# Fourteen operand tiles begin 16 to 240 bytes further on, each at a place of its own

## The chip, the cores and the metric

The kernel runs on one core of a Trainium2 chip. The time is device microseconds from launch to end, as the median of several executions. Four engines compute: PE (TensorE, matrix products into PSUM; its weight loads are shown as PEld), DVE (VectorE), ACT (ScalarE) and POOL (GpSimd). SP (SyncE) and POOL issue transfers.

## The reference

One encoder block on 512 tokens of 1024 channels. After a norm, one projection feeds three mixers: a bidirectional mLSTM, a neighbourhood attention on an 8 x 64 grid, and a cross-attention into 256 memory tokens. Their results are merged by gates. The end of the block, which matters here, is

```python
        merged = g_ml * (y_ml @ w_br_ml[l]) + g_na * (y_na @ w_br_na[l]) + g_xa * (y_xa @ w_br_xa[l])
        x = x + merged @ w_out[l]
        x = x + conv_glu_ffn(rms_norm(x, ffn_norm_g[l]), w_ffn_up[l], w_ffn_conv[l], b_ffn_conv[l], w_ffn_down[l])
    return rms_norm(x, final_norm_g)
```

with `conv_glu_ffn(h) = (gelu(dwconv3(a)) * u) @ w_down`, where `a` and `u` are the halves of `h @ w_up`, 2816 channels each. All data are float32.

## The kernel before, in words

Data is kept turned: channels on the 128 partitions, the 512 tokens along the free dimension. A matrix product therefore has a 128 x 128 block of weights as stationary operand and a 128 x 512 slice of data as moving operand. To keep float32 accuracy, each operand is split into a high part (rounded to the type fp32r) and a low part (the rest), and each product is made of three matmuls into one PSUM bank, in `mm3` (lines 213 to 215): high weights by high data, high weights by low data, low weights by high data. The program loads the weights for each of the three anew, so every matmul has its weight load, which overlaps the matmul before.

Weights come in blocks of up to 1088 floats per partition (`emit_raw`, three buffers), one DMA each on SP's queue. `emit_split` cuts a block into halves of up to 576 floats, high by ACT (line 195) and low by DVE (line 196), four buffers of each. Three blocks ahead are loaded and one ahead is split.

The large data tiles come from one pool of 15 buffers, `unit` (line 130): 2112 floats wide, of which four slices of 512 floats hold data and 64 floats are left over. 2112 floats are 33 x 256 bytes, a weight half of 576 floats is 9 x 256, a raw block of 1088 floats is 17 x 256. A slice of data lies 2048 bytes behind the slice before, a block of weights 512 bytes behind the block before. So, modulo 256 bytes, a unit's slices and the weights' blocks all begin at one place. There are two exceptions, both for 256 columns: `HI256 = 48` floats, 192 bytes, are left free ahead of the high weights of the third token-major block (line 189, where the weights are the moving operand), and ahead of the high weights of the last two output tiles (`lastw`, line 169).

The end of the program is written out in its final order, and the framework adds the semaphores:

- The gates' products are summed in two units. `split_act` (lines 219 and 220: ACT makes the high part, DVE the low one) writes the merged sum into four units, `mhu` (line 1227): high and low of k = 0 to 3, then high and low of k = 4 to 7. They are the moving operand of the output projection, the loop over 8 output tiles f.
- In that loop each tile gets the residual added (line 1244) and is split into four units, `h2` (line 1236), in the same arrangement. They are the moving operand of both halves of the up projection.
- The feed-forward is done in two halves of 11 channel tiles (`for hh in range(2)`, line 1389). Each half takes six units, `gu` (line 1390): three for the high part, three for the low. For each of its 11 tiles there are two up products (`ua`, `uu`, 8 k each), a convolution of three taps, a gelu, a product with `u`, and a split into `gu`. After that the down projection of the half takes `gu` as moving operand: 8 output tiles of 11 k in the first half; in the second half 5 of them, and then `last_tiles`, which works on halves of the tokens and uses `gu` on either side.

Of the kernel before, what the change touches and what calls it, by code (L numbers as in the profile page):

```python
# [12 lines left out]
F32R = mybir.dt.float32r  # L13
# [97 lines left out]
def hybrid_block(ctx, tc, xg, xT, memT, wflat, vecs, gbias, nabias, outa, outb, outc):  # L111
# [14 lines left out]
    def nm(s):  # L126
        uid[0] += 1
        return f"{s}_{uid[0]}"

    def unit(dt=F32):  # L130
        return up.tile([P, UNIT], dt, tag="unit", name=nm("u"))

    def scr(n=512):
        return sp.tile([P, S], F32, tag="scr", name=nm("s"))[:, :n]
# [4 lines left out]
    def mmps():  # L139
        return mmp.tile([P, 512], F32, tag="mm", name=nm("mm"))  # L140
# [60 lines left out]
    def weights(key):  # L201

        i, _, n = BINDEX[key]
        while st["raw"] <= min(i + RAW_AHEAD, len(BLOCKS) - 1):
            emit_raw(st["raw"])
            st["raw"] += 1
        while st["split"] <= min(i + SPLIT_AHEAD, len(BLOCKS) - 1):
            emit_split(st["split"])
            st["split"] += 1
        return split.pop(i)  # L210

    def mm3(ps, lh, ll, rh, rl, start, stop):
        PE.matmul(ps, lh, rh, start=start, stop=False)  # L213
        PE.matmul(ps, lh, rl, start=False, stop=False)  # L214
        st["mm"] = PE.matmul(ps, ll, rh, start=False, stop=stop).ins  # L215

    def split_act(h, l, src, scale=1.0):

        A.activation(h, src, AF.Copy, scale=scale)  # L219
        V.scalar_tensor_tensor(l, src, scale, h.bitcast(F32), op0=ALU.mult, op1=ALU.subtract)  # L220
# [6 lines left out]
    def vcol(name, i):  # L227
        o = VEC[name] + i
        return vec[:, o:o + 1]
# [75 lines left out]
    def folded(acc, ntok):  # L305

        lo, hi = slice(0, P // 2), slice(P // 2, P)
        t, parts = scr(ntok), sp.tile([P, S], F32R, tag="scr", name=nm("s"))[:, :ntok]
        A.activation(t[lo], acc[hi], AF.Copy)
        V.tensor_tensor(t[lo], acc[lo], t[lo], op=ALU.add)  # L310
        A.activation(parts[lo], t[lo], AF.Copy)
        V.tensor_tensor(parts[hi], t[lo], parts[lo].bitcast(F32), op=ALU.subtract)
        return (parts,)

    def square_sums(parts, ntok, pool=atps):

        ps = pool()
        for i, p in enumerate(parts):
            st["mm"] = PE.matmul(ps[:, :ntok], onesr, p, start=i == 0, stop=i == len(parts) - 1).ins
        return ps  # L320
# [12 lines left out]
    def rstd_wide(ps, ntok, tag, n=D):  # L333

        v, y = scr(ntok), scr(ntok)
        rb = cp.tile([P, ntok], F32, name=f"rb_{tag}", tag=f"rb{ntok}", bufs=1) if tag else scr(ntok)
        A.activation(v, ps[:, :ntok], AF.Ln, scale=1.0 / n)
        A.activation(y, v, AF.Exp, scale=-0.5)
        V.scalar_tensor_tensor(v, ps[:, :ntok], -0.5 / n, y, op0=ALU.mult, op1=ALU.mult)
        V.tensor_tensor(v, v, y, op=ALU.mult)  # L340
        V.scalar_tensor_tensor(rb, v, 1.5, y, op0=ALU.add, op1=ALU.mult)
        return rb
# [52 lines left out]
    def proj(key, XHs, XLs, n=S, at={}, ps=None):  # L395

        ws = weights(key)
        k0 = 0 if ps is None else 1
        if ps is None:
            ps = mmps()  # L400
        for k in range(k0, KT):
            mm3(ps[:, :n], ws[k][0], ws[k][1], XHs[k], XLs[k], k == 0, k == KT - 1)
            if k in (1, 3, 5):
                flush()
            if k in at:
                at[k]()
        return ps
# [46 lines left out]
    def conv(ps, rbt, w, b, i, n):  # L454

        pad = pads[npad[0] % 2]
        npad[0] += 1
        V.tensor_tensor(pad[:, 1:513], ps, rbt, op=ALU.mult)  # L458
        t1 = scr()
        A.activation(t1, pad[:, 0:512], AF.Identity, scale=vcol(w, i), bias=vcol(b, i))  # L460
        V.scalar_tensor_tensor(t1, pad[:, 1:513], vcol(w, n + i), t1, op0=ALU.mult, op1=ALU.add)  # L461
        V.scalar_tensor_tensor(t1, pad[:, 2:514], vcol(w, 2 * n + i), t1, op0=ALU.mult, op1=ALU.add)  # L462
        return t1
# [38 lines left out]
    for c in range(3):  # L502
# [10 lines left out]
        for t in range(NT):  # L513
# [3 lines left out]
            if c < 2:  # L517
                o = 16 if c == 0 else 0
# [589 lines left out]
    def step(n=1):  # L1108
        quota[0] += n
        while quota[0] >= 1 and gens:  # L1110
            try:
                next(gens[0])
                quota[0] -= 1
            except StopIteration:
                gens.pop(0)
        if not gens:
            quota[0] = 0.0
# [67 lines left out]
    for br in range(3):  # L1185
# [19 lines left out]
        for fp in range(4):  # L1205
# [18 lines left out]
                    V.scalar_tensor_tensor(tg[i], tg[i], 1.0, ps, op0=ALU.add, op1=ALU.mult)  # L1224
                    V.tensor_tensor(mgv(f), mgv(f), tg[i], op=ALU.add)
            step(1)
    mhu = [unit(F32R) for _ in range(4)]
    GH = [mhu[k // 4 * 2][:, (k % 4) * S:(k % 4 + 1) * S] for k in range(KT)]
    GL = [mhu[k // 4 * 2 + 1][:, (k % 4) * S:(k % 4 + 1) * S] for k in range(KT)]
    for k in range(KT):  # L1230
# [2 lines left out]

    x2u = [unit(), unit()]
    x2 = [x2u[f // 4][:, (f % 4) * S:(f % 4 + 1) * S] for f in range(KT)]
    h2 = [unit(F32R) for _ in range(4)]
    HH = [h2[k // 4 * 2][:, (k % 4) * S:(k % 4 + 1) * S] for k in range(KT)]
    HL = [h2[k // 4 * 2 + 1][:, (k % 4) * S:(k % 4 + 1) * S] for k in range(KT)]
    acc2 = cp.tile([P, S], F32, name="acc_2", tag="acc", bufs=1)
# [147 lines left out]
            SY.dma_start(outc[:, LF * P:], o[:, LF * P:D])  # L1387

    for hh in range(2):
        gu = [unit(F32R) for _ in range(6)]  # L1390
        UH = [gu[k // 4][:, (k % 4) * S:(k % 4 + 1) * S] for k in range(HF)]
        UL = [gu[3 + k // 4][:, (k % 4) * S:(k % 4 + 1) * S] for k in range(HF)]
        for j in range(HF):
            f = HF * hh + j
            if f == 0:
                wa, wu = weights(("ua", f)), weights(("uu", f))
                pa, pu = mmps(), mmps()
                x2sum = folded(acc2, S)
                for k in range(KT):
                    if k < KT - 1:  # L1400
                        mm3(pa, wa[k][0], wa[k][1], HH[k], HL[k], k == 0, False)
                for k in range(KT - 1):
                    mm3(pu, wu[k][0], wu[k][1], HH[k], HL[k], k == 0, False)
                k = KT - 1
                mm3(pa, wa[k][0], wa[k][1], HH[k], HL[k], False, True)
                rb2 = rstd_wide(square_sums(x2sum, S), S, "2")
                mm3(pu, wu[k][0], wu[k][1], HH[k], HL[k], False, True)
                pa1 = proj(("ua", 1), HH, HL)
                pu1 = proj(("uu", 1), HH, HL)
            else:  # L1410
                pa = pa1 if f == 1 else proj(("ua", f), HH, HL)
            c = conv(pa, rb2, "ffw", "ffb", f, FT)
            sq = scr()
            A.activation(sq, c, AF.Square)
            V.scalar_tensor_tensor(sq, sq, GC, c, op0=ALU.add, op1=ALU.mult)  # L1415
            A.activation(sq, sq, AF.Tanh, scale=GK)  # L1416
            V.scalar_tensor_tensor(c, sq, 1.0, c, op0=ALU.add, op1=ALU.mult)  # L1417
            G.tensor_tensor(c, c, rb2, op=ALU.mult)  # L1418
            if f > 0:
                pu = pu1 if f == 1 else proj(("uu", f), HH, HL)  # L1420
            V.tensor_tensor(c, pu, c, op=ALU.mult)  # L1421
            split_act(UH[j], UL[j], c, 0.5)
        for f in range(KT if hh == 0 else LF - 1):
            ws = weights(("dn", hh, f, 0)) + weights(("dn", hh, f, 1))
            ps = mmps()
            for k in range(HF):
                mm3(ps, ws[k][0], ws[k][1], UH[k], UL[k], k == 0, k == HF - 1)
            V.tensor_tensor(x2[f], ps, x2[f], op=ALU.add)  # L1428
            if hh == 1:
                if f == 0:  # L1430
                    with tc.issue_after(A.activation(acc3, x2[f], AF.Square).ins):
                        A.preload_act_table_set("natural_log_exp_and_others")
                else:
                    sq = scr()
                    A.activation(sq, x2[f], AF.Square)
                    G.tensor_tensor(acc3, acc3, sq, op=ALU.add)
                A.activation(x2[f], x2[f], AF.Copy, scale=vcol("fin_g", f))
        if hh == 1:
            last_tiles(UH, UL)
# [114 lines left out]
```

## Time and profile before

| | |
|---|---|
| median of 3 runs | 873.77 us (873.48 to 873.80) |
| profiled execution: span from first to last instruction | 871.2 us |
| PE busy | 865.8 us, 99% of the span, 4287 matmuls |
| DVE, ACT, POOL busy | 594.7, 467.8, 125.4 us |
| mean granted TensorE clock | 1.000 |
| DMA | 99.81 MB, 115 GB/s |

The page gives the span of the profiled execution and no other time for it; the span is the time between first and last instruction, and the runs' times hold what lies around it as well. The chain that ended last is followed back from the last instruction. In the list of groups a line is that of the helper that recorded the instruction, so all split products stand under lines 213 to 215. In the timeline each row has the start in us from the span's start and the duration; PE's rows overlap, since matmuls are pipelined, and the distance from start to start is what a matmul costs. Where that distance is worked out over many rows, the first and the last of them are shown.

### The profile page before, as it was taken

The page shows a single profiled execution, that of the slowest core. Times are in us where ns is not written, and L with a number is a line of the kernel's source. Part 1 is how long each engine was busy: PE and PEld are TensorE (multiplying, and loading weights), DVE is VectorE, ACT ScalarE, POOL GpSimd, SP SyncE. Part 2 cuts the span into 40 slices and gives each one's busy share as a digit, 9 for nine tenths or more (in the row PEclk, how much of TensorE's full clock was granted, in tenths as well). Part 3 has the DMA queues.
Part 4 walks back from the last instruction along what each step waited for, and adds up shares of the span by engine and source line. Part 5 has one row for each costly group of instructions (what it writes and reads, how often), then busy time and mean ns, then how long its engine had stood idle before and what let it go on. Part 6 is the DMA issues. An engine that isn't in the chain of part 4 may idle for free.

```text
span 871.2 us, 12230 instructions
## 1 busy us (share of the span) xinstructions
PE 865.8 (99%) x4287; PEld 733.9 (84%) x4287; DVE 594.7 (68%) x1292; ACT 467.8 (54%) x981; POOL 125.4 (14%) x202
## 2 busy tenths in 40 slices
PE   9999999999999999999999999999999999999997
PEld 7898889888888888888888888888888888888887
DVE  7794698997477768897676558776633466666534
ACT  7563577764355658897534455444422344444532
POOL 0101100000344370600000002111100011111010
PEclk9999999999999999999999999999999999999999
DMA  8324643533343453533223433323233323232412
GB/s 281 101 75 147 196 140 89 169 107 115 93 132 82 113 146 112 160 116 122 99 96 109 144 109 97 98 96 98 78 98 113 102 96 97 96 98 87 141 35 97
DMA packets 39421, 99.81 MB, mean 115 GB/s; under 512 B 5688, under 2 KB 13880, under 8 KB 39360
## 3 DMA queue, kind: packets, MB, share of 16 engines
q1 hardware_dynamic: 31568, 92.32, 32.6%
q0 software_dynamic: 7360, 6.32, 3.4%
q8 instruction: 34, 0.56, 0.3%
q10 hardware_dynamic: 432, 0.39, 0.1%
q14 instruction: 27, 0.22, 0.1%
HBM read 94.80 MB, written 4.21 MB: 114 GB/s over the span
## 4 chain that ended last, share of the span: by engine, by line
PE 98%; DVE 1%; issue 0%; ACT 0%; POOL 0%; POOLq 0%
PE mm L213 29%; PE mm L215 29%; PE mm L214 29%; PE at L214 2%; PE at L213 2%; PE at L215 2%; PE at L982 1%; PE at L963 1%; PE at L944 0%; PE at L945 0%; PE at L765 0%; PE at L813 0%; PE at L1070 0%; PE at L243 0%; PE mm L422 0%
## 5 line engine op out<-in xcount | busy, mean ns | idle before, releaser
L213 PE MATMUL mm<-u,wh 128*128 128x512 f32 (+1 forms) x1072 | 414.3, 386 | 0.0
L215 PE MATMUL mm<-u,wl 128*128 128x512 f32 (+1 forms) x1072 | 411.8, 384 | 0.0
L214 PE MATMUL mm<-u,wh 128*128 128x512 f32 (+1 forms) x1072 | 411.5, 384 | 0.0
L195 ACT ACTIVATE wh<-wr 128x512 fp32r<-128x512 f32 (+2 forms) x298 | 184.2, 621 | 219.9 <-PE mm L214 177.2
L196 DVE TENSOR_TENSOR wl<-wr,wh 128x512 fp32r<-128x512 f32 (+3 forms) x300 | 203.4, 681 | 88.5 <-ACT wh L195 86.4
L215 PEld LDWEIGHTS mm<-u,wl 128*128 128x128 f32 x1072 | 201.3, 188 | 40.3 <-DVE wl L196 0.4
L213 PEld LDWEIGHTS mm<-u,wh 128*128 128x128 f32 x1072 | 201.5, 188 | 39.0 <-ACT wh L195 0.4
L214 PEld LDWEIGHTS mm<-u,wh 128*128 128x128 f32 x1072 | 201.5, 188 | 38.5
L1418 POOL TENSOR_TENSOR s<-s,rb 128x512 f32<-128x512 f32 x22 | 38.2, 1736 | 401.7 <-DVE s L1417 238.9
L540 POOL DMA_DIRECT2D u<-nav_d x128 | 62.5, 535 | 70.5 <-DVE X L220 24.3
L219 ACT ACTIVATE u<-s 128x512 fp32r<-128x512 f32 x26 | 16.4, 632 | 56.4 <-DVE s L1421 56.3
L1421 DVE TENSOR_TENSOR s<-mm,s 128x512 f32<-128x512 f32 x22 | 15.2, 690 | 23.9 <-POOL s L1418 23.9
L460 ACT ACTIVATE s<-pad,vec 128x512 f32<-128x512 f32 x30 | 24.4, 813 | 9.7 <-DVE pad L458 9.7
L220 DVE SCALAR_TENSOR_TENSOR u<-s,u 128x512 fp32r<-128x512 f32 x26 | 19.1, 733 | 14.8 <-ACT u L219 14.5
L461 DVE SCALAR_TENSOR_TENSOR s<-pad,vec,s 128x512 f32<-128x512 f32 x30 | 22.5, 750 | 5.5 <-ACT s L460 5.5
L1417 DVE SCALAR_TENSOR_TENSOR s<-s,s 128x512 f32<-128x512 f32 x22 | 15.2, 691 | 13.4 <-ACT s L1416 13.3
L462 DVE SCALAR_TENSOR_TENSOR s<-pad,vec,s 128x512 f32<-128x512 f32 x30 | 22.5, 750 | 0.9
L1416 ACT ACTIVATE s<-s 128x512 f32<-128x512 f32 x22 | 13.9, 632 | 14.9 <-DVE s L1415 14.9
L1196 DVE TENSOR_TENSOR s<-mm,rb_x 128x512 f32<-128x512 f32 x16 | 11.0, 689 | 13.8 <-PE mm L215 13.7
L458 DVE TENSOR_TENSOR pad<-mm,rb 128x512 f32<-128x512 f32 x22 | 15.1, 690 | 6.4 <-PE mm L215 6.2
L1428 DVE TENSOR_TENSOR u<-mm,u 128x512 f32<-128x512 f32 x13 | 9.0, 692 | 14.6 <-PE mm L215 14.6
L214 PE MATMUL mm<-wl,u 128*128 128x512 f32 x48 | 18.7, 390 | 0.0
(352 smaller groups left out, 1053.3 us busy)
## 6 DMA issues: line engine op xcount, KB each, us to landing
wr<-wflat SPq DMA_DIRECT2D x141, 512.0 KB, 3.3
nab<-nabias SPq DMA_DIRECT2D x16, 256.0 KB, 2.7
u<-nav_d POOLq DMA_DIRECT2D x128, 32.0 KB, 2.8
s<-xT SPq DMA_DIRECT2D x15, 256.0 KB, 4.0
wr<-wflat SPq DMA_DIRECT2D x14, 192.0 KB, 2.4
nav_d<-nv POOLq DMA_DIRECT2D x8, 256.0 KB, 2.5
R<-rd SPq DMA_DIRECT2D x8, 256.0 KB, 4.6
wr<-wflat SPq DMA_DIRECT2D x2, 544.0 KB, 3.4
```

The lines of the kernel that those rows point to most:

```text
L195: A.activation(h[:, u:v], src, AF.Copy)
L196: V.tensor_tensor(l[:, u:v], src, h[:, u:v].bitcast(F32), op=ALU.subtract)
L213: PE.matmul(ps, lh, rh, start=start, stop=False)
L214: PE.matmul(ps, lh, rl, start=False, stop=False)
L215: st["mm"] = PE.matmul(ps, ll, rh, start=False, stop=stop).ins
L219: A.activation(h, src, AF.Copy, scale=scale)
L220: V.scalar_tensor_tensor(l, src, scale, h.bitcast(F32), op0=ALU.mult, op1=ALU.subtract)
L460: A.activation(t1, pad[:, 0:512], AF.Identity, scale=vcol(w, i), bias=vcol(b, i))
L461: V.scalar_tensor_tensor(t1, pad[:, 1:513], vcol(w, n + i), t1, op0=ALU.mult, op1=ALU.add)
L462: V.scalar_tensor_tensor(t1, pad[:, 2:514], vcol(w, 2 * n + i), t1, op0=ALU.mult, op1=ALU.add)
L540: G.dma_start(vw[r * 32:(r + 1) * 32, i * 256:(i + 1) * 256], nav_v[hf, r, CW[b]:CW[b] + 32, hp * 256:(hp + 1) * 256])
L1418: G.tensor_tensor(c, c, rb2, op=ALU.mult)
```

## The change

Fourteen units are used from an offset on, instead of from their first byte. The offsets are, in floats, 40, 56, 8, 4 for the merged gates, 24, 48, 32, 16 for the normalised residual, and 28, 44, 20, 12, 52, 60 for the first feed-forward half: all different, all multiples of 16 bytes, from 16 to 240 bytes. The slices keep their distance of 2048 bytes, and the 64 spare floats of a unit take the offset up. The units of the second feed-forward half keep their place (offset 0), and so do all weights. The instructions, their order and their sizes stay the same.

```diff
-    mhu = [unit(F32R) for _ in range(4)]
+    mhu = [u[:, o:] for u, o in zip([unit(F32R) for _ in range(4)], (40, 56, 8, 4))]
     GH = [mhu[k // 4 * 2][:, (k % 4) * S:(k % 4 + 1) * S] for k in range(KT)]
     GL = [mhu[k // 4 * 2 + 1][:, (k % 4) * S:(k % 4 + 1) * S] for k in range(KT)]
...
-    h2 = [unit(F32R) for _ in range(4)]
+    h2 = [u[:, o:] for u, o in zip([unit(F32R) for _ in range(4)], (24, 48, 32, 16))]
     HH = [h2[k // 4 * 2][:, (k % 4) * S:(k % 4 + 1) * S] for k in range(KT)]
     HL = [h2[k // 4 * 2 + 1][:, (k % 4) * S:(k % 4 + 1) * S] for k in range(KT)]
...
     for hh in range(2):
-        gu = [unit(F32R) for _ in range(6)]
+        gu = [u[:, o:] for u, o in zip([unit(F32R) for _ in range(6)], (28, 44, 20, 12, 52, 60) if hh == 0 else (0,) * 6)]
         UH = [gu[k // 4][:, (k % 4) * S:(k % 4 + 1) * S] for k in range(HF)]
         UL = [gu[3 + k // 4][:, (k % 4) * S:(k % 4 + 1) * S] for k in range(HF)]
```

## The prediction

> **What bounds the kernel now.** The page is read first, from its busy shares (part 1) over the slices (part 2) to the chain that ended last (part 4) and the costliest groups (part 5).
>
> ```profile
> span 871.2 us, 12230 instructions
> PE 865.8 (99%) x4287; PEld 733.9 (84%) x4287; DVE 594.7 (68%) x1292; ACT 467.8 (54%) x981; POOL 125.4 (14%) x202
> ...
> PEclk9999999999999999999999999999999999999999
> ...
> PE 98%; DVE 1%; issue 0%; ACT 0%; POOL 0%; POOLq 0%
> ...
> L213 PE MATMUL mm<-u,wh 128*128 128x512 f32 (+1 forms) x1072 | 414.3, 386 | 0.0
> L215 PE MATMUL mm<-u,wl 128*128 128x512 f32 (+1 forms) x1072 | 411.8, 384 | 0.0
> L214 PE MATMUL mm<-u,wh 128*128 128x512 f32 (+1 forms) x1072 | 411.5, 384 | 0.0
> ```
>
> TensorE never runs dry: 98% of the chain is its own matmuls, the clock is at its full grant in every slice, and the three lines of mm3 show no idle time. So the time is the number of matmuls times the distance from the start of one to the start of the next. That distance is what the change can touch. The mean durations of 384 to 386 ns don't show it, since consecutive matmuls overlap; the timeline does. Next, then, the table by stretches places the four stages whose moving data is shifted, and the timeline of PE inside them gives the distance.
>
> ```profile
> core 0: us, PE busy (x) PEld busy (x) DVE busy (x) ACT busy (x) POOL busy (x), PEclk, DMA share, GB/s
> 459.80:503.50 43.70, 43.70 (x195) 36.18 (x194) 26.42 (x41) 19.21 (x32) 0.00 (x0) 1.00 0.38 126
> 503.50:623.40 119.90, 119.90 (x531) 99.28 (x530) 85.52 (x126) 59.75 (x95) 16.66 (x10) 1.00 0.30 95
> 623.40:683.30 59.90, 59.90 (x266) 49.61 (x265) 21.86 (x34) 15.03 (x26) 1.79 (x1) 1.00 0.34 106
> 683.30:803.00 119.70, 119.70 (x530) 99.12 (x529) 80.69 (x119) 55.63 (x87) 17.95 (x10) 1.00 0.29 92
> ```
>
> ```profile
> start us, us, engine line op out<-in xcount [idle before <-releaser]
> 519.96 0.39 PE L215 MATMUL mm<-u,wl 128*128 128x512 f32 x1
> ...
> 559.86 0.39 PE L214 MATMUL mm<-u,wh 128*128 128x512 f32 x1
> ```
>
> In order: output projection, up projection of the first half, down projection of the first half, up projection of the second half; PE is busy for the whole of each. Between the two timeline rows lie 176 steps of one matmul each: 39.90 us / 176 = 226.7 ns for 512 columns, with DVE and ACT at work beside it and no trace of them.
>
> **The change, part by part.** It adds and removes no instruction, no transfer and no wait; only the addresses of 14 tiles move. Who reads them from TensorE follows from the loops. The merged gates (mhu) are the moving operand of the output projection: 8 tiles x 8 k x 3 = 192 matmuls. The normalised residual (h2) is that of both up projections: 44 x 8 x 3 = 1056. The first feed-forward half (gu, first turn) is that of the first down projection: 8 x 11 x 3 = 264. Together 1512 matmuls, all of 512 columns, out of a stretch of 343 us (459.8 to 803.0). 1512 x 226.7 ns = 342.8 us, so nothing else lies in it.
>
> What the shift does to one matmul is the whole question. Before, units are 33 x 256 bytes wide, weight tiles 9 x 256, and slices start every 512 or 2048 bytes, so the moving slice of each of these matmuls and the weight tile that is loaded for the next begin at the same place modulo 256 bytes. Afterwards the moving data lies 16 to 240 bytes past the weights. The trace has two kinds of matmul that bear on it, neither the same as the changed one.
>
> First, 256 columns. The memory keys run with moving data and weights at one place; in the third token-major block, and in the last tiles, the high halves of the weights lie 192 bytes further on (HI256 = 48 floats).
>
> ```profile
> start us, us, engine line op out<-in xcount [idle before <-releaser]
> 144.11 0.28 PE L214 MATMUL mm<-u,wh 128*128 128x256 f32 x1
> ...
> 145.31 0.28 PE L215 MATMUL mm<-u,wl 128*128 128x256 f32 x1
> ```
>
> ```profile
> start us, us, engine line op out<-in xcount [idle before <-releaser]
> 82.23 0.28 PE L214 MATMUL at<-wl,u 128*128 128x256 f32 x1
> ...
> 92.71 0.28 PE L213 MATMUL at<-wh,u 128*128 128x256 f32 x1
> ```
>
> At one place: 10 steps in 1.20 us, 120.0 ns each. Moved apart: 90 steps in 10.60 us, 117.8 ns. So the place counts, by 2.2 ns. The two widths also give the bare price of a column: (226.7 - 120.0) / 256 = 0.417 ns, so 512 columns cost 213.4 and 256 cost 106.7, and at one place each matmul carries 13.3 ns on top, whatever its width. This steady 13.3 is a settled state, which the second kind shows.
>
> Second, 512 columns at one place, but just after something of another shape (transposes of 128 columns) has broken the stream.
>
> ```profile
> start us, us, engine line op out<-in xcount [idle before <-releaser]
> 118.50 0.39 PE L214 MATMUL mm<-u,wh 128*128 128x512 f32 x1
> ...
> 119.89 0.39 PE L214 MATMUL mm<-u,wh 128*128 128x512 f32 x1
> ```
>
> ```profile
> start us, us, engine line op out<-in xcount [idle before <-releaser]
> 250.85 0.39 PE L214 MATMUL mm<-u,wh 128*128 128x512 f32 x1
> ...
> 252.93 0.39 PE L214 MATMUL mm<-u,wh 128*128 128x512 f32 x1
> ```
>
> ```profile
> start us, us, engine line op out<-in xcount [idle before <-releaser]
> 326.11 0.39 PE L214 MATMUL mm<-u,wh 128*128 128x512 f32 x1
> 326.34 0.39 PE L215 MATMUL mm<-u,wl 128*128 128x512 f32 x1
> 326.57 0.40 PE L213 MATMUL mm<-u,wh 128*128 128x512 f32 x1
> 326.81 0.39 PE L214 MATMUL mm<-u,wh 128*128 128x512 f32 x1
> ...
> 327.50 0.39 PE L214 MATMUL mm<-u,wh 128*128 128x512 f32 x1
> 327.72 0.39 PE L215 MATMUL mm<-u,wl 128*128 128x512 f32 x1
> ```
>
> The first steps are uneven: 230, 230 and 240 ns between the written rows of the third episode, where the rows are rounded to 10. The three episodes have 6, 9 and 6 steps in 1.39, 2.08 and 1.39 us: 4.86 / 21 = 231.4 ns. After five to nine such steps the stream falls into 226.7 and stays there (the 176 steps above). I read this as two streams of reads, moving data and next weights, that settle against each other when both walk through memory from the same place; unsettled, a matmul of 512 columns takes 4.7 ns more.
>
> What a shifted 512-column matmul takes is not in the trace; it is bounded. Below: 213.4 ns, no overhead at all, 1512 x -13.3 = -20.1 us. Above: the longest step that the third episode writes, 240 ns, 1512 x 13.3 = +20.1 us. I take the 231.4 of the unsettled steps, because they are the nearest row in width, which matters here: the shifted 256-column stream, whose two reads also walk apart, never shows a settled step size over its 90 steps, so I expect the shift to keep the long ones from settling too. The sum: 1512 x (231.4 - 226.7) ns = +7.1 us. Span 871.2 + 7.1 = 878.3. The page gives no other time for this execution; the median of the runs, 873.77, stands 2.6 us above its span, so the median becomes 880.9. By the spread of the three episodes (231.1 to 231.7), of the 14 places among themselves, and of a share that settles after all, the likeliest case alone runs from 877 to 885.
>
> The writers of the shifted tiles are ACT and DVE, at the lines of split_act.
>
> ```profile
> L220 DVE SCALAR_TENSOR_TENSOR u<-s,u 128x512 fp32r<-128x512 f32 x21 | 15.6, 743 | 12.7 <-ACT u L219 12.6
> L219 ACT ACTIVATE u<-s 128x512 fp32r<-128x512 f32 x21 | 13.3, 633 | 53.6 <-DVE s L1421 53.6
> ```
>
> I cost them at nothing: a tile of the feed-forward takes 48 matmuls, 10.9 us, against 1.4 us for the pair, and PE waits for neither anywhere in these stretches. If both became half slower, 0.7 us a tile would vanish in DVE's and ACT's idle time. Only where a stage needs the last slice at once (623 and 459 us) could it show, and there other products stand in between or it happens once: at most 0.7 us each. The weights' split and their DMAs don't move, and a slower PE leaves them more time.
>
> [...]
>
> **The rivals.** *Apart is better at 512 columns as well.* The mechanism is the one that the 256-column rows show: two reads that start from one place collide, and moving one of them away takes part of the collision off. Its place is the same 1512 matmuls. Its price: overhead 117.8 - 106.7 = 11.1 instead of 13.3 ns, 1512 x -2.2 = -3.3 us, median 870.4; if all three products of a k were moved apart, rather than the two that use the high half in those rows, half as much again, -5.0 us, 868.8. For it speaks that the rows are of a steady stream, not of a disturbed one; against it, that unsettled 512-column steps cost more than settled ones, while at 256 columns the settled ones are the dear ones, so that the sign need not carry over. It decides as soon as the mean step falls below 226.7.
>
> *The place doesn't matter at this width.* Then the 226.7 ns stay, and the time is 873.8. The uneven steps after a break would have to come from the break alone. A mixture of good and bad places that cancels gives the same time; it needs +4.7 and -2.2 ns in a proportion of about one to two.
>
> *Far dearer.* If most of the places sit at the 235 to 240 ns of single steps, 1512 x 9 to 13 = +14 to +20 us, 887 to 894.
>
> **How the numbers follow.** Unsettled steps, as summed: 0.52, 880.9. Apart is better: 0.34, 870.4. No difference: 0.09, 873.8. Far dearer: 0.05. The range leaves out the far case, and the upper end of the likeliest and the lower end of the second with it, together about 2 in 10: 868.5 to 885. A difference of 0.2%, 1.7 us, is about what a measurement of this kernel can tell from no change (its three runs lie within 0.04%). Faster by more than that: 0.33, nearly all of the second case; within it: 0.10; slower: 0.57, the first and the last.
>
> **What the changed profile would show.** Right: in the stretch from 460 us on, the timeline steps of lines 213 to 215 no longer repeat 226.7 but scatter around 231, the four stages are 0.9, 2.5, 1.2 and 2.5 us longer (192, 528, 264 and 528 x 4.7 ns), and the second down projection, whose data keeps its place, is back at 226.7 after a few steps; the first 460 us are unchanged to 0.2 us. Each of the 14 tiles has a place of its own, so its steps can be told apart by k: if the steps differ between the first four k and the rest, the distance to the weights matters, not the loss of settling. Wrong: steps below 226.7 in all stages (the second case), or the same 226.7 (the third); or new idle time of PE before a stage, which would point to the writers.

## The result, and the profile after

The changed kernel takes 881.30 us (median of 4 runs, 880.75 to 881.45), beside 873.62 us for the kernel before (median of 4 runs, 872.86 to 873.80). The ratio is 1.009, with a 95% interval of 1.0076 to 1.0105: 0.9% slower. The forecast was 880.9 us, inside a range of 868.5 to 885.

The page of the changed kernel, in the order in which the page before was read: busy shares, granted clock, chain, costliest groups (count, then busy us and mean ns of one, then idle time before).

```profile
span 879.5 us, 12230 instructions
PE 874.1 (99%) x4287; PEld 735.2 (84%) x4287; DVE 612.6 (70%) x1292; ACT 468.5 (53%) x981; POOL 117.3 (13%) x202
...
PEclk9999999999999999999999999999999999999999
...
PE 98%; DVE 1%; issue 0%; ACT 0%; POOL 0%; POOLq 0%
...
L213 PE MATMUL mm<-u,wh 128*128 128x512 f32 (+1 forms) x1072 | 417.1, 389 | 0.0
L215 PE MATMUL mm<-u,wl 128*128 128x512 f32 (+1 forms) x1072 | 413.9, 386 | 0.0
L214 PE MATMUL mm<-u,wh 128*128 128x512 f32 (+1 forms) x1072 | 413.9, 386 | 0.0
```

The shape is that of before: PE is 99% busy at full clock, is 98% of the chain, and its three lines have no idle time. The span is 8.3 us longer and PE's busy time grows by just that, 865.8 to 874.1. The mean durations rise by 2 to 3 ns only, because 568 of the 1072 matmuls of each line were not shifted; the busy sums of the three lines rise by 2.8 + 2.1 + 2.4 = 7.3 us, so the loss to look for is of about that size. The table by stretches, with the same bounds as before:

```profile
core 0: us, PE busy (x) PEld busy (x) DVE busy (x) ACT busy (x) POOL busy (x), PEclk, DMA share, GB/s
459.80:503.50 43.70, 43.70 (x190) 35.36 (x189) 27.08 (x42) 20.38 (x33) 0.00 (x0) 1.00 0.37 121
503.50:623.40 119.90, 119.90 (x519) 97.22 (x518) 87.35 (x123) 57.71 (x91) 14.88 (x10) 1.00 0.29 95
623.40:683.30 59.90, 59.90 (x261) 48.66 (x260) 24.78 (x37) 16.33 (x27) 1.29 (x1) 1.00 0.33 102
683.30:803.00 119.70, 119.70 (x518) 97.08 (x517) 86.72 (x113) 51.80 (x82) 12.87 (x10) 1.00 0.28 90
```

In equal time PE starts 190, 519, 261 and 518 matmuls, where it started 195, 531, 266 and 530. (The stages begin later in this execution, so the stretches cut them at slightly other places.) PE is busy for the whole of every stretch: nothing waits, each matmul takes longer. The timeline of PE gives the distance, first and last row of three streams: the output projection, the up projection of the first half (the stretch that the prediction quoted), and the second down projection, whose data was not moved.

```profile
462.05 0.40 PE L215 MATMUL mm<-u,wl 128*128 128x512 f32 x1
...
502.93 0.39 PE L214 MATMUL mm<-u,wh 128*128 128x512 f32 x1
...
519.85 0.39 PE L214 MATMUL mm<-u,wh 128*128 128x512 f32 x1
...
559.94 0.39 PE L213 MATMUL mm<-u,wh 128*128 128x512 f32 x1
...
812.98 0.39 PE L214 MATMUL mm<-u,wh 128*128 128x512 f32 x1
...
839.96 0.39 PE L213 MATMUL mm<-u,wh 128*128 128x512 f32 x1
```

These are 40.88 us over 176 steps, 232.3 ns; 40.09 us over 173 steps, 231.7 ns, against 226.7 before; and 26.98 us over 119 steps, 226.7 ns. The two traces hold the same matmuls in nearly the same order, so each stage can be measured from the start of its first matmul to the start of the next stage's first:

| stage (matmuls) | before, us | after, us | difference | forecast |
|---|---|---|---|---|
| output projection (192) | 43.52 | 44.59 | +1.07 | +0.9 |
| up projection, first half (528) | 119.91 | 122.54 | +2.63 | +2.5 |
| down projection, first half (264) | 59.84 | 61.01 | +1.17 | +1.2 |
| up projection, second half (528) | 119.68 | 122.31 | +2.63 | +2.5 |
| sum | | | +7.50 | +7.1 |

The other 0.8 us of the 8.3 lies in the first microseconds, long before anything that was moved. The first 512-column matmul, of line 213, starts at 4.74 us before and 5.33 after, the next of line 214 at 5.08 and 5.97, as PE's timeline of the kernel before and then that of the kernel after have them:

```profile
4.74 0.40 PE L213 MATMUL mm<-u,wh 128*128 128x512 f32 x1
4.97 0.28 PE L431 MATMUL mm<-u,wh 128*128 128x256 f32 x1
5.08 0.39 PE L214 MATMUL mm<-u,wh 128*128 128x512 f32 x1
```

```profile
5.33 0.63 PE L213 MATMUL mm<-u,wh 128*128 128x512 f32 x1
...
5.97 0.63 PE L214 MATMUL mm<-u,wh 128*128 128x512 f32 x1
6.40 0.44 PE L215 MATMUL mm<-u,wl 128*128 128x512 f32 x1
6.68 0.40 PE L213 MATMUL mm<-u,wh 128*128 128x512 f32 x1
6.91 0.40 PE L214 MATMUL mm<-u,wh 128*128 128x512 f32 x1
```

The rows show what it is: in the kernel after, a 512-column matmul takes 0.43 us until 6.4 us (5.97 to 6.40) and 0.23 us from 6.68 on; in the kernel before it takes 0.23 us at 4.74 already. The clock records in the two traces begin, with full clock, at 6.48 us and at 3.90 us. In the traces of the first six experiments below they begin between 3.96 and 6.24 us, and the output projection starts 0.1 to 0.6 us later than in the trace of before; the 6.24 and the 0.6 belong to the first of them, which takes as long as the kernel before. The medians of the runs differ by 7.68 us, little more than the 7.50 of the stages. So I take the 0.8 us for scatter between executions, most of it in when the full clock comes; what sets that moment was not looked for.

One side effect is off the path. Two groups of DVE and POOL, in the kernel before and then after:

```profile
L196 DVE TENSOR_TENSOR wl<-wr,wh 128x512 fp32r<-128x512 f32 (+3 forms) x300 | 203.4, 681 | 88.5 <-ACT wh L195 86.4
L1418 POOL TENSOR_TENSOR s<-s,rb 128x512 f32<-128x512 f32 x22 | 38.2, 1736 | 401.7 <-DVE s L1417 238.9 <-PE mm L215 162.8
```

```profile
L196 DVE TENSOR_TENSOR wl<-wr,wh 128x512 fp32r<-128x512 f32 (+3 forms) x300 | 221.7, 741 | 94.5 <-ACT wh L195 92.2
L1418 POOL TENSOR_TENSOR s<-s,rb 128x512 f32<-128x512 f32 x22 | 30.3, 1379 | 416.6 <-DVE s L1417 416.6
```

DVE's share of the weight split takes 60 ns more in the mean and POOL's multiplication 357 ns less. In the experiments this goes with the step of the up projections (the distance from one matmul's start to the next): DVE is busy for 595 to 596 us where that is 226.7 or 228.9 ns, for 612 where it is 232 to 233, and for 608 in the scan of distances, which has both. So I take it to follow from the slower PE; that was not tested by itself. The writers of the shifted tiles, lines 219 and 220, kept their price (632 and 744 ns a full slice against 633 and 743). PE waited for none of this.

### The profile page after: what moved, and what is told of

It reads as the page before. It is cut to its first block, busy times and chain, and to the rows that moved or that the text cites. A ratio compares the mean times of both kernels' runs of the same rounds, so it can differ in the third digit from the quotient of the medians.

```text
span 879.5 us, 12230 instructions
## 1 busy us (share of the span) xinstructions
PE 874.1 (99%) x4287; PEld 735.2 (84%) x4287; DVE 612.6 (70%) x1292; ACT 468.5 (53%) x981; POOL 117.3 (13%) x202
## 4 chain that ended last, share of the span: by engine, by line
PE 98%; DVE 1%; issue 0%; ACT 0%; POOL 0%; POOLq 0%
PE mm L213 29%; PE mm L214 29%; PE mm L215 29%; PE at L214 2%; PE at L213 2%; PE at L215 2%; PE at L982 1%; PE at L963 1%; PE at L944 0%; PE at L945 0%; PE at L765 0%; PE at L813 0%; PE at L1070 0%; PE at L243 0%; PE mm L422 0%
## 5 line engine op out<-in xcount | busy, mean ns | idle before, releaser
L196 DVE TENSOR_TENSOR wl<-wr,wh 128x512 fp32r<-128x512 f32 (+3 forms) x300 | 221.7, 741 | 94.5 <-ACT wh L195 92.2
L1418 POOL TENSOR_TENSOR s<-s,rb 128x512 f32<-128x512 f32 x22 | 30.3, 1379 | 416.6 <-DVE s L1417 416.6
L1417 DVE SCALAR_TENSOR_TENSOR s<-s,s 128x512 f32<-128x512 f32 x22 | 15.2, 692 | 13.4 <-ACT s L1416 13.3
L215 PE MATMUL mm<-wh,u 128*128 128x512 f32 x48 | 18.7, 390 | 0.0
```

The costliest lines, as they stand in the source:

```text
L196: V.tensor_tensor(l[:, u:v], src, h[:, u:v].bitcast(F32), op=ALU.subtract)
```

## The experiments

The theory going in is the prediction's: what costs is that the moving data and the next weights no longer lie at one place modulo 256 bytes, so that the stream cannot settle. The rivals differ in what about the places counts: the absolute place, the distance between the two, the number of weight columns read, or the order of places from one matmul to the next. Distances are between data and weights, modulo 256 bytes (where the weights were moved, they lie that far beyond the data; where the data was, the data beyond them); a step is the mean distance from start to start in the stretch of the up projection, if nothing else is said. "Settled" is the mean over the last 12 or more steps of a block, in the trace's own nanoseconds, once the steps repeat. Lines that begin with a minus are those of the changed kernel; an edit that only adds lines goes into the kernel before.

**Weights moved along.** All 14 tiles at 24 floats (96 bytes; the lines of mhu and gu are changed likewise), and the split weights of the four stages 24 floats further on as well.

```diff
-    h2 = [u[:, o:] for u, o in zip([unit(F32R) for _ in range(4)], (24, 48, 32, 16))]
+    h2 = [u[:, o:] for u, o in zip([unit(F32R) for _ in range(4)], (24,) * 4)]
...
+                if key[0] in ("out", "ua", "uu") or key[:2] == ("dn", 0):
+                    h, l = h[:, 24:], l[:, 24:]
```

> All fourteen tiles begin 24 floats (96 bytes) further on, and so do the high and low weights of the four stages that read them, so moving data and weights are at one place again, but at another absolute one than in the kernel before. Theory 1 (it is the distance between moving data and weights that counts, and at distance 0 the stream settles): 226.7 ns a step in all four stages, time as before, 873.7 us within 1 us. Rival (data off its old absolute place costs, wherever the weights lie): about 231.5 ns a step, 881 us.

Measured: 873.56 us beside 873.55, ratio 1.0001 (0.9992 to 1.0011). The timeline of this kernel, in the same stretch:

```profile
519.96 0.39 PE L217 MATMUL mm<-u,wl 128*128 128x512 f32 x1
...
559.85 0.39 PE L216 MATMUL mm<-u,wh 128*128 128x512 f32 x1
```

39.89 us over 176 steps is 226.7 ns. With the whole shift in place and its distance to the weights taken away, the whole loss is gone. So the absolute place of the data is cleared (at the one place tried), and so are its writers: it is the place of the data relative to the weights.

**One distance instead of fourteen.** As above without the weights' two lines (24 floats, 96 bytes), and the same with 32 floats (128 bytes); mhu and gu as h2.

```diff
-    h2 = [u[:, o:] for u, o in zip([unit(F32R) for _ in range(4)], (24, 48, 32, 16))]
+    h2 = [u[:, o:] for u, o in zip([unit(F32R) for _ in range(4)], (24,) * 4)]
```

> All fourteen tiles begin 24 floats (96 bytes) further on, the weights keep their place: one constant distance instead of fourteen. Theory 1 (only equal places settle): about 231 ns a step, 880 to 882 us. Rival A (it is the change of place from matmul to matmul that keeps the stream from settling, a constant distance settles as well): 226.7 ns, 873.7 us. Rival B (two reads that start together collide, apart is better): below 226.7 ns, 868 to 872 us.

```diff
-    h2 = [u[:, o:] for u, o in zip([unit(F32R) for _ in range(4)], (24, 48, 32, 16))]
+    h2 = [u[:, o:] for u, o in zip([unit(F32R) for _ in range(4)], (32,) * 4)]
```

> As the run before, with 32 floats (128 bytes). If the pattern of places repeats every 128 bytes, this distance is as good as none: 226.7 ns a step and 873.7 us. If it repeats every 256 bytes, 128 bytes is the farthest distance there is: by theory 1 about 231 ns and 880 to 882 us, by the rival that apart is better the lowest step of all, below 226.7.

Measured: 883.61 us (ratio 1.0116, 1.01 to 1.0132) and 882.11 us (1.0101, 1.0083 to 1.012). The timeline at 96 bytes:

```profile
520.02 0.39 PE L213 MATMUL mm<-u,wh 128*128 128x512 f32 x1
...
559.92 0.39 PE L213 MATMUL mm<-u,wh 128*128 128x512 f32 x1
```

39.90 us over 171 steps is 233.3 ns; at 128 bytes it is 39.97 us over 172 steps, 232.4 ns. 1512 x 6.6 = 10.0 us, the whole of what was measured. And this is where the theory of "not settling" falls: at 96 bytes the stream does settle. In the first down projection the matmuls of lines 213, 214 and 215 take 230, 232 and 238 ns, nearly without scatter, over 88 of each. A shifted stream finds its steady pattern; the pattern is dearer. At 128 bytes the price is still there, so what counts does not repeat every 128 bytes.

**All distances in one run.** The data lies as before; the weights of up tile f are moved by 16 bytes times (f mod 16), those of the output projection in the low half only, those of the first down projection in the high half only.

```diff
+                oh = ol = 0
+                if key[0] in ("ua", "uu"):
+                    oh = ol = 4 * (key[1] % 16)
+                elif key[0] == "out":
+                    ol = 8 * key[1]
+                elif key[:2] == ("dn", 0):
+                    oh = 8 * key[2]
+                h, l = h[:, oh:], l[:, ol:]
```

> The data tiles are as in the kernel before, the weights move: in the two up projections the high and low weights of tile f begin 4 x (f mod 16) floats further on, so one run has every distance from 0 to 240 bytes; in the output projection the low weights alone move by 8 x f floats, in the first down projection the high weights alone by 8 x f. Theory 1: the tiles with f mod 16 = 0 take 226.7 ns a step, all others 229 to 234. If the pattern repeats every 128 bytes, f = 8 too takes 226.7. Rival (each distance has a step of its own, and some are better than none): a curve over f with tiles clearly below 226.7, down to 220 or less. The whole: 877 to 881 us by theory 1.

Measured: 880.4 us, in one run. The settled mean by distance, in the up projections:

| distance, bytes | 0 | 16 | 32 to 64 | 80 | 96 | 112 to 160 | 176 | 192 | 208 | 224 | 240 |
|---|---|---|---|---|---|---|---|---|---|---|---|
| step, ns | 226.7 | 226.7 | 233.3 | 232.0 | 234.3 | 233.3 | 230.0 | 228.9 | 231.7 | 233.3 | 228.3 |

The timeline of this kernel at 16, 32 and 192 bytes (20 steps in 4.53 us, 21 in 4.90, 17 in 3.89):

```profile
518.91 0.39 PE L222 MATMUL mm<-u,wh 128*128 128x512 f32 x1
...
523.44 0.39 PE L221 MATMUL mm<-u,wh 128*128 128x512 f32 x1
...
529.88 0.40 PE L222 MATMUL mm<-u,wh 128*128 128x512 f32 x1
...
534.78 0.40 PE L222 MATMUL mm<-u,wh 128*128 128x512 f32 x1
...
703.06 0.39 PE L221 MATMUL mm<-u,wh 128*128 128x512 f32 x1
...
706.95 0.39 PE L223 MATMUL mm<-u,wl 128*128 128x512 f32 x1
```

No distance is below 226.7, and every one settles into a short repeating pattern of its own. Moving only the high or only the low weights gives 229 to 233.5, over the later steps of each tile. It is a curve over the distance, not two states.

**Each product's data with the weights that are loaded behind it.** High data and high weights at 0, low data and low weights both 24 floats on. The line of mhu is changed as that of h2, and the offsets of gu are three times 0 and three times 24.

```diff
-    h2 = [u[:, o:] for u, o in zip([unit(F32R) for _ in range(4)], (24, 48, 32, 16))]
+    h2 = [u[:, o:] for u, o in zip([unit(F32R) for _ in range(4)], (0, 24, 0, 24))]
...
+                if key[0] in ("out", "ua", "uu") or key[:2] == ("dn", 0):
+                    l = l[:, 24:]
```

> High data and high weights keep their place, low data and low weights of the four stages both begin 24 floats (96 bytes) further on. Theory 1a (what counts is the distance between the data that streams and the weights that are loaded meanwhile, those of the next matmul): in the order high by high, high by low, low by high this distance is 0 in each step, so 226.7 ns and 873.7 us. Rival (the distance to the matmul's own weights, or any change of place from step to step, counts): two of three steps are apart, about 231 ns and 880 to 882 us.

Measured: 876.59 us beside 873.33, ratio 1.0038 (1.0023 to 1.0053), between the two expectations. The timeline:

```profile
519.88 0.39 PE L216 MATMUL mm<-u,wh 128*128 128x512 f32 x1
...
559.94 0.39 PE L217 MATMUL mm<-u,wl 128*128 128x512 f32 x1
```

40.06 us over 175 steps is 228.9 ns: 231, 232 and 224 for the three products. So the sameness of a matmul's data and of the weights loaded during it (in the kernel before the next weights load for 0.19 us from 519.97 us on, beside the matmul that starts at 519.96) does not settle the price by itself. Something else in the order counts too, the matmul's own weights or the change of place from one matmul to the next; the two were not told apart. Neither expectation had the value.

**The up projections undone.** The change, with the normalised residual back at offset 0.

```diff
-    h2 = [u[:, o:] for u, o in zip([unit(F32R) for _ in range(4)], (24, 48, 32, 16))]
+    h2 = [u[:, o:] for u, o in zip([unit(F32R) for _ in range(4)], (0, 0, 0, 0))]
```

> The change without the normalised residual: h2 is back at offset 0, merged gates and first feed-forward half stay shifted. If the stages add up, the up projections return to 226.7 ns, and there remain 192 x (232.1 - 226.7) + 264 x (231.1 - 226.7) ns = 2.2 us: 875.8 us. If the loss of one stage depended on another (a write to a shifted tile, a late engine), it would be off by more than 1 us.

Measured: 875.81 us beside 873.33, ratio 1.003 (1.0017 to 1.0043). Its timeline, in the output projection and the up projection:

```profile
461.87 0.39 PE L213 MATMUL mm<-u,wh 128*128 128x512 f32 x1
...
501.81 0.40 PE L214 MATMUL mm<-u,wh 128*128 128x512 f32 x1
...
519.85 0.39 PE L214 MATMUL mm<-u,wh 128*128 128x512 f32 x1
...
559.97 0.39 PE L214 MATMUL mm<-u,wh 128*128 128x512 f32 x1
```

172 steps of 232.2 ns, then 177 of 226.7: the stage that is undone is back, the other keeps its price. The stages add up: the two that stay shifted were 1.07 + 1.17 = 2.2 us dearer in the changed kernel, and 2.5 us are left here.

**Fewer weight columns, other widths.** The kernel before, with blocks of extra matmuls between the two halves. They write a bank that nothing reads, so this kernel is longer by the blocks, and its whole time is not compared; it and the next two kernels ran once each. Each block repeats the three products of a split multiplication, with data and weights taken from the normalised residual at set places, 30 matmuls to a place; weights of 128, 64 or 32 columns, data of 256 to 512.

```diff
...
+    def probe(n, cols, mh, ml, wh, wl, reps=8):
+        ps = atps()
+        for i in range(reps):
+            o = i % 3 * S
+            H, L = h2[0][:, o + mh:o + mh + n], h2[1][:, o + ml:o + ml + n]
+            hi, lo = h2[2][:, o + wh:o + wh + cols], h2[3][:, o + wl:o + wl + cols]
+            PE.matmul(ps[:cols, :n], hi, H, start=True, stop=False)
+            PE.matmul(ps[:cols, :n], hi, L, start=False, stop=False)
+            PE.matmul(ps[:cols, :n], lo, H, start=False, stop=True)
...
```

> The kernel before with a probe added ahead of the second feed-forward half: blocks of 30 matmuls into a bank that nobody reads, on the residual's tiles, with 128, 64 or 32 columns of weights, weights 0 to 192 bytes past the moving data, and 256 to 512 columns of moving data. Theory 2 (the 13.3 ns a step beyond 213.4 are the price of loading the next weights out of the same memory): at distance 0 the price goes with the weights' columns, 226.7, 220.0, 216.7 ns for 128, 64, 32; apart it is irregular for 128 and shrinks too. Rival (a fixed pause of each matmul): 226.7 for all three. Width: at distance 0 always 13.3 ns over 0.417 ns a column (120.0, 146.7, 173.4, 200.0 for 256, 320, 384, 448); at 128 bytes less than that for 256, more for 512, the sign turning between.

Its timeline at distance 0, with 128 columns of weights and then with 32 (24 steps in 5.44 us, 21 in 4.87; the first steps of the second are not settled yet):

```profile
684.34 0.39 PE L1398 MATMUL at<-u,u 128*128 128x512 f32 x1
...
689.78 0.39 PE L1398 MATMUL at<-u,u 128*128 128x512 f32 x1
...
698.52 0.40 PE L1397 MATMUL at<-u,u 128*32 128x512 f32 x1
...
703.39 0.39 PE L1397 MATMUL at<-u,u 128*32 128x512 f32 x1
```

Settled at distance 0, 128, 64 and 32 columns take 226.7, 229.7 and 231.8 ns: there fewer weights to read make the step dearer, where a price by the column of weights had 220 and 216.7. That rival falls. But it is no rule that fewer columns cost more: with the weights 96 bytes on, the three take 234.3, 226.6 and 230.3 ns. The rows at 64 columns, 96 bytes on (12 steps in 2.72 us):

```profile
756.28 0.39 PE L1397 MATMUL at<-u,u 128*64 128x512 f32 x1
...
759.00 0.39 PE L1397 MATMUL at<-u,u 128*64 128x512 f32 x1
```

With 32 columns the place hardly counts (230.3 to 231.8 at six distances); with 64 it ranges from 226.6 to 233.4, with 128 from 226.7 to 234.3. By width, settled at distance 0 and at 128 bytes: 256 columns 120.0 and 118.7, 320 columns 146.7 and 146.6, 384 columns 173.3 and 176.0, 448 columns 206.7 and 204.0, 512 columns 226.7 and 233.6. So the sign of the effect does turn between 320 and 384 columns, and then again at 448 and at 512. One thing here contradicts the scan of distances: 16 bytes apart takes 233.2 ns in these blocks, and 226.7 there.

**Random places.** The same blocks, 24 matmuls each, at 64 sets of places drawn at random (low data, high and low weights; high data at 0), all of 512 and 128 columns.

```diff
+PROBES = [(512, 128, 0, 32, 44, 0, 8), (512, 128, 0, 56, 28, 4, 8), (512, 128, 0, 20, 12, 44, 8),
...
+          (512, 128, 0, 52, 36, 32, 8)]
```

> The same probe with 64 drawn sets of places for low data, high weights and low weights (multiples of 16 bytes below 256, high data at 0), 512 columns, 24 matmuls a set. Theory 1: 228 to 235 ns for nearly all, 226.7 only where every step has its data and the next weights within 16 bytes of each other, none below 226.7. Rival (some arrangement of places collides less than equal places): sets below 226.7 ns, which would be a faster kernel.

The settled steps, over the last 12 of each block, run from 226.67 to 235.6 ns; the mean of the 64 is 231.5 and the median 231.2, and 18 sets lie at 233.3 or above. Not one is below 226.67. Three reach it, with places that are not equal: low data, high and low weights at 20, 0, 60 floats, at 20, 60, 60 and at 40, 60, 32. One of the cheapest and one of the dearest in the timeline (20, 0, 60, 12 steps in 2.72 us; 44, 44, 32, 12 steps in 2.83):

```profile
986.00 0.39 PE L1399 MATMUL at<-u,u 128*128 128x512 f32 x1
...
988.72 0.40 PE L1399 MATMUL at<-u,u 128*128 128x512 f32 x1
```

```profile
830.13 0.40 PE L1398 MATMUL at<-u,u 128*128 128x512 f32 x1
...
832.96 0.40 PE L1398 MATMUL at<-u,u 128*128 128x512 f32 x1
```

So equal places are enough for the lowest step, and not needed for it; and no arrangement seen beats the kernel before.

**Standing operands.** Blocks of 30 matmuls in which one operand does not walk: the weights are one column, read 128 times, or the moving data is one column, read 512 times; and blocks whose moving data is gathered in pieces from further apart.

```diff
...
+            if "w1" in kind:
+                wt = h2[2][:, o + w:o + w + 1].to_broadcast([P, P])
+            if "m1" in kind:
+                x = h2[0][:, o + m:o + m + 1].to_broadcast([P, S])
+            if kind[:1] == "b":
+                n, step = [int(v) for v in kind[1:].split("x")]
+                x = h2[0][:, m:m + S // n * step].rearrange("p (a b) -> p a b", b=step)[:, :, :n]
...
```

> The kernel before with another probe at the same spot: 20 blocks of 30 matmuls of 512 columns by 128 columns of weights. In some the weights are one column read 128 times (w1), so their read stands still; in some the moving data is one column read 512 times (m1); in others the moving data is gathered in pieces (32 pieces of 16 to 2 pieces of 256 floats, at several strides). If the 13 to 20 ns beyond 213.4 come from two reads that walk and meet, a standing read of either kind brings the step to about 214 to 217 ns and the place no longer counts. If they come from the moving read alone, standing weights still take 226 to 234 and only standing data falls to 214 to 217. If they are a fixed pause of each matmul, all blocks take 226.7 or more. A gathered form below 226.7 would be a faster layout.

PE's timeline, with equal rows drawn together (start of the first, from there to the end of the last, count): walking operands at one place, standing weights, standing data, and data gathered in 32 pieces of 16 floats, 64 apart.

```profile
684.16 6.05 PE L1407 MATMUL at<-u,u 128*128 128x512 f32 x26
...
691.66 5.71 PE L1407 MATMUL at<-u,u 128*128 128x512 f32 x24
...
719.14 5.78 PE L1407 MATMUL at<-u,u 128*128 128x512 f32 x26
...
773.12 6.16 PE L1407 MATMUL at<-u,u 128*128 128x512 f32 x25
```

One matmul of these lasts 389, 394, 379 and 402 ns by the groups, so the steps are (6.05 - 0.39) / 25 = 226.4, (5.71 - 0.39) / 23 = 231, (5.78 - 0.38) / 25 = 216 and (6.16 - 0.40) / 24 = 240 ns; from the trace's starts, settled, 226.7, 231.1, 215.8 and 240.0. Standing data takes 215.8 at both places of the weights that were tried, and when they stand too. Standing weights take 231.1 at both places tried, 231.5 with the data 96 bytes on, and 231 when the data alternates between two tiles at different places. Gathered in pieces of 64 floats or more, at strides of 128, 256 or 512 floats, the data costs the plain 226.7; pieces of 32 floats, 128 apart, 236.4; strides of 68, 80 and 132 floats 233.3, of 144 floats 240.0. The gathered forms at 226.7 are those that run through the same places modulo 256 bytes (64 floats) in the same order as data in one piece; every form with another order is dearer. That is in line with places counting modulo 256 bytes.

That turns the picture round. The overhead of 13.3 ns that the prediction found belongs almost wholly to the walk of the moving data: 215.8 - 213.4 = 2.4 ns are left when it stands (213.4 is the prediction's estimate, from the steps of 226.7 and 120.0 ns at 512 and 256 columns). It is not all the price of a collision with the weights, for with weights that read one column over and over the stream is still at 231. The walk of the weights moves it from there in both ways: at the data's place down to 226.7, at 96 bytes up to 234.3, in the random sets to somewhere between 226.67 and 235.6. With 32 columns of weights the stream is at 230 to 232 again.

## Why the prediction was right, and where its reasons were not

**The bound, the count, the place of the loss: right.** The four stages took 7.50 of the forecast 7.1 us, each within 0.2 us of its line; the second down projection is back at 226.7 ns, no idle time appeared before PE, and the writers cost nothing, as summed. The 0.8 us at the start was not in the sum, which had the first 460 us unchanged to 0.2 us; it is not of the change's doing, since the moved tiles are first read after 459 us.

**The term of the sum: right in size.** 231.4 ns was taken for a shifted matmul; the mean over the four stages is 231.6 (226.7 and 7.50 us over 1512). That the two agree so closely is luck: single steps in the shifted stages run from 224 to 239 ns, and the whole effect is 5 ns. In the first down projection, by the starts in the trace, the three products take 228 to 230 ns in the mean with the data of the first four k, 237, 233 and 224 with the next four, repeating in each group of three, and 233 to 234 with the last three. The text had said what this would mean: steps that differ between the first four k and the rest speak for the distance, against the loss of settling. They do.

**"I expect the shift to keep the long ones from settling": this step failed.** Shifted streams settle, at 96 bytes into 230, 232 and 238 ns without scatter. The row that the step rested on was misread: in nanoseconds, the shifted 256-column stream from 82.23 us on repeats every 18 steps (121, 118, 117, 118, 115, 117, 122, ... ns), five times over in its 90, so it had settled too, into a longer pattern. (The two rows shown for it are 89 steps in 10.48 us, not 90 in 10.60; the quotient is the same 117.8.) What the unsettled steps after a break and the shifted steady streams have in common is their level. Standing weights run at 231.1, 32-column weights at 230 to 232, and the 64 random sets, from 226.67 to 235.6, have a mean of 231.5: about 231 is what 512 walking columns cost with the weights out of play or on average over their places. The three episodes after a break lie at the same level; that they have the same cause was not tested, and as the reason given was wrong, the right number is in part luck. It would not have served for one place alone: at 96 bytes the forecast is 2.9 us too low, and for the paired places 3.8 us too high (1512 x (231.4 - 228.9) ns).

**"Two streams of reads that settle against each other": half right.** The place relative to the weights is what counts, as the weights moved along show (226.7 ns with both 96 bytes on, 233.3 with the data alone). But the weights are not the source of most of the overhead; the walk of the moving data is (215.8 ns when it stands, 231.1 when the weights do), and the weights take some of it off or add to it, by their place (226.7 at the data's place, 234.3 at 96 bytes beyond it). That two reads settle or collide was my reading of such steps; no trace shows the reads themselves.

**The rival that apart is better, given 0.34, is refuted** at 512 columns: none of 16 distances and 64 random sets goes below 226.67. The caution that the sign need not carry over from 256 columns was the right one, and the widths show it: apart is cheaper at 256 (120.0 to 118.7) and dearer at 384 and 512. **No difference** is refuted by the ratio's interval. **Far dearer** needs most places at 235 to 240; the dearest single place in the scan takes 234.3.

**What stays open.** Why the walk of the moving data costs 11 ns at the best places (226.7 - 215.8) and 24 in the dearest gathered forms (240.0 - 215.8), and by what rule a set of places gets its pattern. That 16 bytes apart took 226.7 ns in the scan, where it followed a stream at distance 0, and 233.2 in the blocks may mean that one set of places has more than one steady pattern, and that what ran before picks it; no run tested this. Equal places are no full account either: three random sets with unequal places, and 64-column weights 96 bytes on, reach the same 226.7. Nor is it settled why 448 columns at one place take 206.7 ns, 6.7 more than the 200 of the other widths' line.

## What to carry to other kernels

Where a stream of 512-column fp32r matmuls is the bound, start moving tiles and weight tiles at the same place modulo 256 bytes; it was the surest way to the lowest step seen with walking data and 128 columns of weights, 226.7 ns, and 1512 matmuls off it cost 3 to 10 us in the kernels above. Test such a placement in a short block of extra matmuls of the very width before the whole kernel is moved, since the sign was another one at 256 columns (120.0 ns at one place, 118.7 at 128 bytes), and read the distance from start to start in the stage itself, not the mean of a line's group, which mixes shifted and unshifted matmuls. And when a number is forecast from a nearby row, ask what else would give that row the same level: here a number was right and its reason was not.

## What the runs showed of the hardware that was not expected

- Moving data that stands still takes 215.8 ns for 512 columns, data that walks 226.7 to 236 in one piece and up to 240.0 when gathered (pieces of 16 floats 64 apart, or of 128 floats 144 apart): the rate of this matmul depends on how its data is addressed, with PE's clock at full grant (1.0 in that run's record).
- Fewer columns of weights made the matmul slower at the data's own place, 226.7, 229.7 and 231.8 ns for 128, 64 and 32 columns, and faster 96 bytes beyond it: 234.3, 226.6 and 230.3 ns.
- Most of these matmul streams fall into a pattern that repeats to within 1 ns (at distance 0 after six to nine uneven steps, 224 to 236 ns, in the three episodes of the kernel before): every 3 steps with the data 96 bytes on (230, 232, 238 ns), every 18 for the shifted 256 columns of the kernel before.
- The streams at distance 0 have settled steps of 120.0, 146.7, 173.3, 206.7 and 226.7 ns for 256 to 512 columns in steps of 64, all of them whole multiples of 6.67 ns (18, 22, 26, 31 and 34). It is an observation of these five only; mixed places give means in between.
